# Five places reordered in a one-core hybrid transformer block

## The chip, the cores and the metric

The kernel runs on one core of one Trainium2 chip. The metric is device microseconds of one launch; a kernel's time is the median of its runs. The engines are named as in the profile: PE (TensorE) multiplies matrices, PEld is its weight load, DVE (VectorE) and ACT (ScalarE) do elementwise work, POOL (GpSimd) does some elementwise work and issues part of the transfers, and SP (SyncE) issues the rest. Each engine works through its own instruction queue in order, and the queues wait for each other through semaphores.

## The reference, cut to what matters

One block of a streaming encoder, for 1024 tokens of width 1024, all in float32:

```python
h = rmsnorm(x, norm_mix_g)
z = h @ w_in                       # one projection, then split
y_a = hgrn2(...)                   # gated recurrence, 4 heads of 128
y_b = fox(...)                     # forgetting attention, 8 heads of 64
y_c = memory(...)                  # attention into 256 memory tokens, 4 heads
gates = sigmoid(gate_logits)       # 3 branches x 1024
merged = sum_i gates_i * (y_i @ w_br_i)
x = x + merged @ w_out
h2 = rmsnorm(x, norm_ffn_g)
a, v = split(h2 @ w_up)            # 2 x 2816
y = gelu(causal_dwconv3(a) + b) * v
out = x + y @ w_down               # the "way down", 2816 -> 1024
```

## The kernel before, in words

Every float32 operand of a product is split into a high part, rounded to the matmul's own type (a cast on ACT, line 120), and a low part, the rest (a subtraction on DVE, line 128). A product is then three matmuls for each 128-deep slice (`mm3`, lines 114 to 116): high by high, high by low, low by high. The matrices are tiled in 128 rows by 512 columns, one bank of the accumulator memory each. Banks come from four rotating tags: `pp` (three), `lg` (two), `tr` (two) and `po` (one).

The large projections (pairs of projection chunks, the way up with `w_up` and the way down with `w_dn`) use a Winograd form of Strassen's scheme: seven products in place of eight for two by two blocks, on sums of blocks. One side's sums are made once and kept split ("families": B11, T1, T2, B22, T3, B21, T4); the other side's operands o1 to o7 are made anew for each unit. In one unit of the way up (`unit`) the products run in the order o1, o2, o3, o4, o5 (T3), o6 (B21), o7 (T4), and copies of half-finished banks (`snap`, line 1215) and final writes (`put`) go between.

The stages in order of time, with the places that the change touches:

- Start (0 to about 90 us): x is loaded in eight chunks `xk`. `x_chunk` makes the scaled and split operands `uh`, `ul` (lines 276, 277). The first two gate chunks and the memory's keys and values are projected meanwhile. `x_norm` squares the rows of x on ACT (line 356; the last one is `late["square"]`). `differences` (line 542) multiplies the eight chunks by their gains in place, on ACT, for the families.
- Dense pairs, then attention into memory and the forgetting attention (about 90 to 677 us). The attention's last head runs beside `hgrn_values`.
- HGRN2 (about 677 to 925 us): `hgrn_prep(h)` projects three things for a head in six halves of 24 matmuls. Each half is taken out of its bank by a multiplication on DVE into a tile `zt` (line 888), and a tanh on ACT writes it on (line 890). `hgrn_mix(h)` is the recurrence: exponentials on ACT, products of the key side on POOL (line 951), of the query side on DVE (line 952), small matmuls, and a norm whose power runs on POOL (`rstd_small`, line 133). The chunks of branch 1 run between the steps of the last head.
- The branches with their gates, `w_out`, the second norm, then the way up: `first_products` and `families` (lines 1285 to 1296) begin it; 22 units follow, with the results `yd` stored to memory.
- Way down: stages A11, S1, S2, S4, S3, A12, A22, each in six steps of up to two 128-deep slices. A step loads a weight and a `yd` piece (line 1406) and splits both (tiles `dwh`, `dwl`, `dbh`, `dbl`).

Space is taken from pools that are opened and closed like a stack. A tile that is laid over one from a closed pool waits for the last use of the old one. A tag has a fixed number of buffers that rotate in program order: `wl2` has five, `wh2` six, `rw` (raw weights of a unit) two, the gate tiles `gt` three (in the pool `gp`, open from the dense stage's end to the branches' end), `zt` one (in the pool `ph`, which lies over the attention's pools).

The order within each engine's queue is made by a scheduler that takes instructions by program order and priority as their inputs come free in its own model of time. `tc.issue_after(ins)` adds an edge without a wait: what the block issues on the engine of `ins` comes behind `ins` in that engine's queue. Instructions of other engines in the block are not bound by it.

The part of the way up's opening that the change adds to:

```python
for name, q, after in (("B22", 3, None), ("T3", 1, "e5"), ("B21", 2, "snap"), ("T4", 0, "snap")):
```

Of the kernel before, what the change touches and what calls it, by code (L numbers as in the profile page):

```python
# [8 lines left out]
F32 = mybir.dt.float32  # L9
# [5 lines left out]
P = 128  # L15
# [55 lines left out]
def tile_block(ctx: ExitStack, tc: tile.TileContext, xT, memT, x_rows, mem_rows, vec, fbias, mats, hmask, w_cm, w_hi, w_fqk, w_fv,  # L71
# [45 lines left out]

    def cast(eng, out, in_):
        if eng is S:
            S.copy(out, in_)  # L120
        elif eng is V:
            V.tensor_copy(out, in_)
        else:
            G.tensor_scalar(out, in_, 1.0, 0.0, ALU.mult, ALU.add)
# [5 lines left out]
    def rstd_small(out, ss, n):  # L130
        w = ss.shape[1]
        V.tensor_scalar(out, ss, 1.0 / n, EPS, ALU.mult, ALU.add)
        G.tensor_tensor(out, out, mhalf[:, :w], ALU.pow)

    wsplit = [S, V]

# [399 lines left out]
    def differences():  # L536

        b = []
        for k in range(4):
            for t in (k, k + 4):  # L540
                with tc.issue_after(late["square"].ins) if t > 3 else nullcontext():
                    S.activation(xk[t], xk[t], AF.Copy, scale=col(C_GX + t))
            b.append([xk[k + 4 * c][:, n * HB:(n + 1) * HB] for c in range(2) for n in range(2)])
        for k, (b11, b12, b21, b22) in enumerate(b):
            V.tensor_sub(b11, b11, b12)
            family_block("T1", k, b11)
        yield
        with tc.issue_after(first_gates.ins):
            for k, (t1, b12, b21, b22) in enumerate(b):
                V.scalar_tensor_tensor(out=t1, in0=t1, scalar=-1.0, in1=b22, op0=ALU.mult, op1=ALU.subtract)  # L550
                family_block("T2", k, t1)
        yield
        with tc.issue_after(first_gates.ins):
            for k, (t2, b12, b21, b22) in enumerate(b):
                V.tensor_sub(b12, b22, b12)
                family_block("T3", k, b12)
        yield
        for k, (t2, b12, b21, b22) in enumerate(b):
            V.scalar_tensor_tensor(out=t4[k], in0=t2, scalar=-1.0, in1=b21, op0=ALU.mult, op1=ALU.subtract)
        pxk.release()  # L560
        home["raw"] = tc.alloc_tile_pool(name="ps2", bufs=1, side="left", reuse_waits="tile")
        new_family(home["raw"], "T4")
        for k in range(4):
            family_block("T4", k, t4[k])
        yield
# [312 lines left out]
    def hgrn_prep(h):  # L878
        ph = state["ph"]
        qt = ph.tile([P, T], F32, tag="hq", name=f"hq_{h}", bufs=2)  # L880
        at = ph.tile([P, T], F32, tag="ha", name=f"ha_{h}", bufs=2)
        gz = ph.tile([P, T], F32, tag="hz", name=f"hz_{h}", bufs=2)
        for what, base, dst in ((0, 4, at), (1, 0, qt), (2, 8, gz)):

            for n, ps in cm_chunk(w_cm[base + h], KC, uh, ul, h == 3 and what == 2):
                sl = slice(n * HB, (n + 1) * HB)
                zt = ph.tile([P, HB], F32, tag="zt", name="zt")
                V.tensor_mul(zt, ps, rx[:, sl])  # L888
                d = dst[:, sl]
                S.activation(d, zt, AF.Tanh, scale=0.5)  # L890
                if what == 0:

                    G.tensor_scalar(d, d, TMIN, c1[:, h:h + 1], ALU.max, ALU.mult)
                else:

                    V.scalar_tensor_tensor(out=d, in0=d, scalar=1.0, in1=zt, op0=ALU.add, op1=ALU.mult)
                yield
        hset[h] = (qt, at, gz)
# [3 lines left out]
    def hgrn_mix(h, ya):  # L902
# [7 lines left out]
        for n in range(2):  # L910
# [103 lines left out]
            rr = ph.tile([P, 4], F32, tag="rr", name="rr", bufs=2)  # L1014
            S.activation(o2, po.rearrange("p (b v) -> p b v", b=4), AF.Square)
            V.reduce_sum(rr, o2, axis=AX.X)
            rstd_small(rr, rr, 4 * P)
            for b in range(4):
                S.activation(o2[:, b, :], po[:, b * P:(b + 1) * P], AF.Copy, scale=rr[:, b:b + 1])
            ptr = ps_tr()  # L1020
# [81 lines left out]
    yc = [[py.tile([P, T], F32R, tag=f"yc{p}{c}", name=f"yc{p}{c}") for c in range(4)] for p in "hl"]  # L1102
    for c in range(4):
        for t, d in zip(yc, ycd):
            G.dma_start(t[c], d[:, c, :].bitcast(F32R))
    run_all(branch(0, yh, yl))
    run_all(branch(2, *yc))
    mh, ml = [], []
# [31 lines left out]

    def operand_parts(h, src):
        l = pl.tile([P, HB], F32R, tag="wl2", name="wl2", bufs=5)
        late["split"] = split(S, h, l, src)
        return h, l

    def first_operands():
# [95 lines left out]
        V.tensor_add(t, a, b)  # L1242
        return t

    def unit(src, put, begun=None, before=None, after=None):


        raw = pw.tile([P, 4, HB], F32, tag="rw", name="rw", bufs=2)
        for i in range(2):
            late["raw"] = G.dma_start(raw[:, 2 * i:2 * i + 2, :], src[:, 2 * i:2 * i + 2, :])  # L1250
        a11, a21, a22, a12 = (raw[:, i, :] for i in range(4))
        if begun:
            x, y, e1, e5, e2, o4 = begun
            o5, o6, o7 = operand(sum_of(3, a11, a21)), operand(a12), operand(a22)
            before()
        else:
            with tc.issue_after(after.ins) if after else nullcontext():
                o1 = operand(a11)
                s1 = sum_of(1, a21, a22)
                o2 = operand(s1)  # L1260
            s2 = sum_of(2, s1, a11)
            x, y, e1, e5, e2 = first_products(o1, o2, operand(s2))
            o4 = operand(sum_of(4, s2, a12))
            o5 = operand(sum_of(3, a11, a21))
        product(y, o4, "B22", False)
        put(0, 1, y, e2)
        if not begun:
            o6 = operand(a12)
        product(x, o5, "T3", False)
        put(1, 1, x, e5)  # L1270
        if not begun:
            o7 = operand(a22)
        z = ps_tr()
        product(z, o6, "B21", True)
        put(0, 0, z, e1)
        product(x, o7, "T4", False)
        put(1, 0, x, None)
# [4 lines left out]
    def families():  # L1282

        for name, q, after in (("B22", 3, None), ("T3", 1, "e5"), ("B21", 2, "snap"), ("T4", 0, "snap")):
            with ExitStack() as order:
                if after:
                    order.enter_context(tc.issue_after(late[after].ins))
                if after == "snap":
                    order.enter_context(tc.issue_after(late["split"].ins))
                for k in range(4):  # L1290
                    late["last"] = family_block(name, k, quarters(k)[q])
            if name == "T3":
                spread(r2, rt2)
        px.release()
        late["pq"] = tc.alloc_tile_pool(name="pq", bufs=1, side="right", reuse_waits="tile")
# [14 lines left out]
                yield  # L1310

    sums = weight_sums()

    for p in range(NF // 2):
        at = []
# [51 lines left out]
                V.tensor_mul(dst, src, dst)  # L1367
            SP.dma_start(yd[:, 2 * c + n, p, :], dst)

        unit(w_up[2 * p + 1], put_v, after=None if p else late["last"])  # L1370
        for _ in range(1 + (1 <= p < 4)):
            next(sums, None)
        t1 = pq.tile([P, HB], F32, tag="ft", name="ft")
# [64 lines left out]
    for a, b, own, first, c, n, sign, last, xq in (  # L1438
# [4 lines left out]
        if not own and first:  # L1443
            ybanks = [ps_lg(), ps_lg(), ps_tr(), ps_tr()]
        dst = banks if own else ybanks
        end = a == "A22"
        held = []
        for i, ks in enumerate(steps):
            eng = G if a == "A11" else SP
            ops = [*parts("w", fetch("w", i, a, eng=eng)), *parts("b", yside(b, i, eng))]  # L1450
            if i == 4 and xq:
                with tc.issue_after(late["sp"].ins) if "sp" in late else nullcontext():
                    x_quarter(*xq)
            held.append((ks, *ops))
            if end and ks is steps[-2]:
                continue
            for m in range(4):
                for kk, h1, l1, h2, l2 in held:
                    for j in range(kk.stop - kk.start):
                        k = kk.start + j  # L1460
                        ms = slice(m * P, (m + 1) * P)
                        mm3(dst[m], h1[:, j, ms], l1[:, j, ms], h2[:, j, :], l2[:, j, :],
                            first and k == 0, k == NP - 1, not first)
                if ks.stop == NP:
                    j, sl = m + 4 * c, slice(n * HB, (n + 1) * HB)
                    d = xb[:, j, sl]
                    (V.tensor_add if sign > 0 else V.tensor_sub)(d, d, dst[m])
                    if last:
                        SP.dma_start(outT[:, j, sl], d)
            held = []  # L1470
# [110 lines left out]
```

## Time and profile before

| what | value |
|---|---|
| runs (3) | median 1764.69 us, 1764.61 to 1765.21 |
| the profiled execution | 1764.18 us |
| its span, first to last instruction | 1762.4 us |
| mean granted PE clock | 0.996 |
| PE busy | 1736.2 us, 99% |
| DVE busy | 1185.8 us, 67% |
| ACT busy | 786.7 us, 45% |
| POOL busy | 334.7 us, 19% |

The profile is one execution. "Busy" counts an engine's instructions; matmuls are pipelined, so a busy PE need not be at its peak. In the view of waits a line says who waited for whom, for how long in total, how often, and the longest time. In the timeline a line has the start, the duration, the engine, the line of the code, the operation, output and input tiles, sizes, and in brackets how long the engine stood idle before and what ended that. In the view of windows each engine has its busy time and number of instructions in a stretch; PEclk is the granted share of TensorE's full clock there.

### The profile page before, as it was taken

How to read it: one execution, taken by the hardware profiler on the slowest of the kernel's cores; microseconds unless marked ns; L12 is line 12 of the kernel's file. 1: busy time of each engine (PE TensorE's matmuls, PEld its weight loads, DVE VectorE, ACT ScalarE, POOL GpSimd, SP SyncE). 2: the span in 40 equal slices, each digit the busy share in tenths (PEclk: the TensorE clock that was granted, in tenths of full speed). 3: DMA queues.
4: the chain of work that ended last, by engine and by line, in shares of the span. 5: the costliest groups of instructions: out<-in, count | busy, mean ns of one | idle time of the engine just before them, and what ended most of it. 6: DMA issues, size and time to landing. Idle time of an engine off the chain costs nothing.

```text
span 1762.4 us, 24530 instructions
## 1 busy us (share of the span) xinstructions
PE 1736.2 (99%) x9069; PEld 1471.4 (83%) x9069; DVE 1185.8 (67%) x2181; ACT 786.7 (45%) x1318; POOL 334.7 (19%) x431
## 2 busy tenths in 40 slices
PE   8999999999999999999989999999999999999998
PEld 6778899989898997888878888788888888778887
DVE  7656445665756567778866755797777877674654
ACT  8633356545555554445331233543343443433332
POOL 1100032443424333334230000111111111100000
PEclk9999999999999999999999999999999999999999
DMA  9533232221212211001226452466454445494772
GB/s 361 178 119 105 83 128 73 76 95 60 91 47 85 84 46 52 25 31 56 77 78 216 153 200 80 136 188 163 139 160 133 119 128 152 144 362 145 238 269 84
DMA packets 83209, 227.36 MB, mean 129 GB/s; under 512 B 9600, under 2 KB 12424, under 8 KB 83088
## 3 DMA queue, kind: packets, MB, share of 16 engines
q1 hardware_dynamic: 65040, 161.29, 26.1%
q0 software_dynamic: 18048, 64.50, 12.6%
q8 instruction: 71, 1.16, 0.3%
q14 instruction: 50, 0.41, 0.1%
HBM read 180.88 MB, written 67.93 MB: 141 GB/s over the span
## 4 chain that ended last, share of the span: by engine, by line
PE 97%; ACT 1%; DVE 1%; DMA 0%; issue 0%; SPq 0%; POOL 0%; DVEq 0%; ACTq 0%
PE pp L115 21%; PE pp L116 21%; PE pp L114 21%; PE lg L115 4%; PE lg L116 4%; PE lg L114 4%; PE tr L114 2%; PE tr L115 2%; PE tr L116 2%; PE lg L970 2%; PE po L836 1%; PE lg L795 1%; PE lg L794 1%; PE po L835 1%; PE po L116 1%; PE po L114 1%
## 5 line engine op out<-in xcount | busy, mean ns | idle before, releaser
L115 PE MATMUL pp<-ul,wh 128*128 128x512 f32 x412 | 165.6, 402 | 0.0
L116 PE MATMUL pp<-uh,wl 128*128 128x512 f32 x412 | 165.4, 401 | 0.0
L114 PE MATMUL pp<-uh,wh 128*128 128x512 f32 x412 | 163.2, 396 | 1.5 <-DVE zt L888 1.5
L115 PE MATMUL pp<-wl,uh 128*128 128x256 f32 (+1 forms) x512 | 145.7, 285 | 0.0
L116 PE MATMUL pp<-wh,ul 128*128 128x256 f32 (+1 forms) x512 | 145.3, 284 | 0.0
L114 PE MATMUL pp<-wh,uh 128*128 128x256 f32 (+1 forms) x512 | 144.7, 284 | 0.0
L120 ACT CAST wh<-s 128x512 fp32r<-128x512 f32 x113 | 68.4, 619 | 152.8 <-PE pp L115 76.8
L120 ACT CAST wh<-raw 128x1024 fp32r<-128x1024 f32 (+2 forms) x76 | 67.5, 890 | 98.9 <-PE pp L115 86.9
L1250 POOL DMA_DIRECT2D rw<-in_w_up x44 | 24.1, 554 | 403.4 <-ACT sqs L1185 169.9
L114 PEld LDWEIGHTS pp<-wh,uh 128*128 128x128 f32 x512 | 96.4, 189 | 1.2
L116 PEld LDWEIGHTS pp<-wh,ul 128*128 128x128 f32 x512 | 96.5, 189 | 0.9
L115 PEld LDWEIGHTS pp<-wl,uh 128*128 128x128 f32 x512 | 96.4, 188 | 0.9
L120 ACT CAST dwh<-wr 128x1024 fp32r<-128x1024 f32 (+1 forms) x42 | 41.1, 980 | 124.6 <-PE tr L115 41.7
L120 ACT CAST wh<-rw 128x512 fp32r<-128x512 f32 x83 | 50.6, 619 | 101.2 <-PE pp L115 59.7
L114 PEld LDWEIGHTS pp<-uh,wh 128*128 128x128 f32 x412 | 78.4, 190 | 17.5 <-DVE zt L888 1.7
L115 PEld LDWEIGHTS pp<-ul,wh 128*128 128x128 f32 x412 | 77.9, 189 | 16.8
L116 PEld LDWEIGHTS pp<-uh,wl 128*128 128x128 f32 x412 | 77.9, 189 | 15.5
L128 DVE TENSOR_TENSOR wl<-raw,wh 128x1024 fp32r<-128x1024 f32 (+2 forms) x76 | 78.4, 1033 | 17.9 <-ACT wh L120 12.7
L128 DVE TENSOR_TENSOR wl<-s,wh 128x512 fp32r<-128x512 f32 x113 | 77.0, 683 | 8.9 <-ACT wh L120 8.9
L128 DVE TENSOR_TENSOR wl<-rw,wh 128x512 fp32r<-128x512 f32 x83 | 55.7, 686 | 29.5 <-PE pp L116 14.1
L951 POOL TENSOR_TENSOR X<-X,kt 128x256 f32<-128x256 f32 x48 | 50.4, 1057 | 124.5 <-ACT X L950 119.5
L128 DVE TENSOR_TENSOR dwl<-wr,dwh 128x1024 fp32r<-128x1024 f32 (+1 forms) x42 | 47.6, 1133 | 39.0 <-ACT dwh L120 39.0
(471 smaller groups left out, 5185.7 us busy)
## 6 DMA issues: line engine op xcount, KB each, us to landing
rw<-in_w_up POOLq DMA_DIRECT2D x44, 512.0 KB, 4.6
sd<-in_w_dn POOLq DMA_DIRECT2D x30, 512.0 KB, 5.9
br<-yd SPq DMA_DIRECT2D x30, 512.0 KB, 5.3
raw<-in_w_cm SPq DMA_DIRECT2D x26, 512.0 KB, 3.4
gd<-gt SPq DMA_DIRECT2D x48, 256.0 KB, 2.0
gt<-gd SPq DMA_DIRECT2D x48, 256.0 KB, 2.8
yd<-fc SPq DMA_DIRECT2D x44, 256.0 KB, 2.5
wr<-sd SPq DMA_DIRECT2D x20, 512.0 KB, 4.4
```

The lines of the kernel that those rows point to most:

```text
L114: PE.matmul(ps, lh, rh, start=first, stop=False, skip_group_check=more)
L115: PE.matmul(ps, lh, rl, start=False, stop=False, skip_group_check=more)
L116: PE.matmul(ps, ll, rh, start=False, stop=last, skip_group_check=more)
L120: S.copy(out, in_)
L128: return (sub or V).tensor_sub(l, src, h.bitcast(F32))
L794: PE.matmul(ps[:, :w], qa[i][:, tsl], kh[i][:, s0:s0 + w], start=True, stop=False)
L795: fox_sets[p][3] = PE.matmul(ps[:, :w], qa[i][:, tsl], kl[i][:, s0:s0 + w], start=False, stop=True)
L835: PE.matmul(o, vhl[:, sb, :], ph[:, src], start=(sb == 0), stop=False)
L836: PE.matmul(o, vhl[:, sb, :], pl[:, src], start=False, stop=last)
L951: G.tensor_mul(Xk, Xk, Kv[:, :, 0, :])
L970: PE.matmul(o[:, b * 64:(b + 1) * 64], X[:, b * P:(b + 1) * P], Xq[:, b * bpb:(b + 1) * bpb, :], start=True, stop=True)
L1250: late["raw"] = G.dma_start(raw[:, 2 * i:2 * i + 2, :], src[:, 2 * i:2 * i + 2, :])
```

## The change

Five edits, from the first place in time to the last:

1. The in-place scalings of x (line 542): before, those of chunks 4 to 7 stood behind the last square in ACT's queue; now all eight do.
2. `hgrn_prep(0)`: its six copies `zt` go to gate tiles (three buffers, already open) in place of the one `zt` buffer of the pool `ph`. Heads 1 to 3 keep `zt`.
3. The eight loads of the memory branch's operands `yc` (line 1105, POOL's queue) are put behind the last power of the HGRN2 norm (`state["norm"]`) in POOL's queue.
4. In the way up's opening, ACT's casts of family B21 come behind the cast of o5, and those of T4 behind the cast of o7.
5. In the last unit of the way up, between products T3 and B21, a new function `down_operands` loads the pieces of the way down's first step (two loads on POOL's queue into an `rw` buffer) and splits them as four operands of 512 columns in `wh2` and `wl2`. The first step of stage A11 uses these and loads and splits nothing itself.

```diff
     def cast(eng, out, in_):
         if eng is S:
-            S.copy(out, in_)
+            return S.copy(out, in_)
...
         for k in range(4):
             for t in (k, k + 4):
-                with tc.issue_after(late["square"].ins) if t > 3 else nullcontext():
+                with tc.issue_after(late["square"].ins):
                     S.activation(xk[t], xk[t], AF.Copy, scale=col(C_GX + t))
...
-                zt = ph.tile([P, HB], F32, tag="zt", name="zt")
+
+                zt = ph.tile([P, HB], F32, tag="zt", name="zt") if h else gate_tile()
                 V.tensor_mul(zt, ps, rx[:, sl])
...
-            rstd_small(rr, rr, 4 * P)
+            state["norm"] = rstd_small(rr, rr, 4 * P)
...
         for t, d in zip(yc, ycd):
-            G.dma_start(t[c], d[:, c, :].bitcast(F32R))
+            with tc.issue_after(state["norm"].ins):
+                G.dma_start(t[c], d[:, c, :].bitcast(F32R))
...
         l = pl.tile([P, HB], F32R, tag="wl2", name="wl2", bufs=5)
-        late["split"] = split(S, h, l, src)
+        late["cast"] = cast(S, h, src)
+        late["split"] = V.tensor_sub(l, src, h.bitcast(F32))
...
-            o5, o6, o7 = operand(sum_of(3, a11, a21)), operand(a12), operand(a22)
+            o5 = operand(sum_of(3, a11, a21))
+            late["o5"] = late["cast"]
+            o6, o7 = operand(a12), operand(a22)
+            late["o7"] = late["cast"]
             before()
...
             o7 = operand(a22)
+        if ahead:
+            ahead()
         z = ps_tr()
         product(z, o6, "B21", True)
...
                 if after == "snap":
                     order.enter_context(tc.issue_after(late["split"].ins))
+                    order.enter_context(tc.issue_after(late["o7" if name == "T4" else "o5"].ins))
...
+    class Blocks:
+
+        def __init__(self, tiles):
+            self.tiles = tiles
+
+        def __getitem__(self, at):
+            return self.tiles[at[1]][:, at[2]]
+
+    def down_operands():
+
+        raw = pw.tile([P, 4, HB], F32, tag="rw", name="rw", bufs=2)
+        G.dma_start(raw[:, 0:2, :], w_dn[:, 0, 0:2, :])
+        G.dma_start(raw[:, 2:4, :], yd[:, 0, 0:2, :])
+        ops = [operand(raw[:, i, :]) for i in (0, 2, 1, 3)]
+        late["down"] = [Blocks([ops[i + 2 * j][q] for j in range(2)]) for i in range(2) for q in range(2)]
...
-        unit(w_up[2 * p + 1], put_v, after=None if p else late["last"])
+        unit(w_up[2 * p + 1], put_v, after=None if p else late["last"],
+             ahead=down_operands if p == NF // 2 - 1 else None)
...
-            ops = [*parts("w", fetch("w", i, a, eng=eng)), *parts("b", yside(b, i, eng))]
+            if a == "A11" and i == 0:
+                ops = late["down"]
+            else:
+                ops = [*parts("w", fetch("w", i, a, eng=eng)), *parts("b", yside(b, i, eng))]
```

More of the change, by code (lines that the diff above doesn't have):

```diff
@@ L132, in rstd_small @@
         V.tensor_scalar(out, ss, 1.0 / n, EPS, ALU.mult, ALU.add)
[L133 removed]
+        return G.tensor_tensor(out, out, mhalf[:, :w], ALU.pow)
     wsplit = [S, V]
@@ L1243, in sum_of, with unit @@
         return t
-    def unit(src, put, begun=None, before=None, after=None):
+    def unit(src, put, begun=None, before=None, after=None, ahead=None):
         raw = pw.tile([P, 4, HB], F32, tag="rw", name="rw", bufs=2)
```

## The prediction

> **What bounds the kernel now.** I read the page first, for the busy shares. PE is the bound, and at most 26 us of its span are not matmuls:
>
> ```profile
> span 1762.4 us, 24530 instructions
> ```
>
> ```profile
> PE 1736.2 (99%) x9069; PEld 1471.4 (83%) x9069; DVE 1185.8 (67%) x2181; ACT 786.7 (45%) x1318; POOL 334.7 (19%) x431
> ```
>
> So a change of order gains only where PE waits. The second view is the list of PE's waits (who waited for whom, us in total, times, longest), whose six longest entries hold most of the idle time:
>
> ```profile
> PE tr L114 <- ACT wh L120: 5.8, 2, 5.3
> PE lg L970 <- POOL X L951: 4.5, 1, 4.5
> PE pp L114 <- ACT wh L120: 2.6, 1, 2.6
> PE pp L115 <- DVE dbl L128: 1.5, 1, 1.5
> PE pp L114 <- DVE zt L888: 1.5, 1, 1.5
> PE po L114 <- ACT gh L120: 1.4, 1, 1.4
> ```
>
> The first is the wait for the first operand after the start, which nothing here touches. The others are five places, each waiting once. Four of them answer to edits 1, 2, 4 and 5; the 4.5 us for POOL's product lie near edit 3.
>
> Third, windows laid behind these places show a second price. The number after POOL's is the granted clock:
>
> ```profile
> 678.31:681.72 3.41, 3.41 (x9) 2.63 (x10) 1.47 (x3) 1.14 (x2) 2.80 (x2) 0.50 0.56 168
> 907.00:913.83 6.83, 6.20 (x30) 6.20 (x31) 2.80 (x5) 1.62 (x5) 2.53 (x3) 0.50 0.01 2
> 1545.30:1548.71 3.41, 3.31 (x8) 2.63 (x9) 3.41 (x5) 0.00 (x0) 1.61 (x3) 0.50 1.01 359
> 1123.10:1126.51 3.41, 3.41 (x23) 3.15 (x24) 3.41 (x6) 2.68 (x5) 0.64 (x2) 1.00 0.20 82
> ```
>
> Behind the `zt` wait and behind the `dbl` wait PE ran 3.41 us at half clock, so each lost 3.41 x 0.5 = 1.7 us more; behind POOL's product it was 6.83 us, a loss of 3.4. The last row lies behind the 2.6 us wait, at full clock: whether a wait trips the clock is not decided by its length alone.
>
> [...]
>
> **Edit 1, scalings of x.** Three of the eight scalings run on ACT between 15 and 25 us, the third directly ahead of the cast for which PE waits:
>
> ```profile
> 15.00:25.00 10.00, 3.34 (x3) 1.00 1.03 410
> ```
>
> ```profile
> 23.96 1.14 ACT L542 ACTIVATE xk<-xk,cv 128x1024 f32<-128x1024 f32 x1
> 25.00 1.03 ACT L120 CAST gh<-raw 128x1024 fp32r<-128x1024 f32 x1
> ```
>
> Its source, the issue on SP and the time from issue to landing of this tile's loads:
>
> ```profile
> 13.84 0.33 SPq L139 DMA_DIRECT2D raw<-in_w_cm  x1
> ```
>
> ```profile
> DMA to landing us min/median/max: 6.6/8.7/10.1
> ```
>
> Without them ACT comes to the cast 3.3 us sooner, at about 21.7. Its source was issued at 13.84 and lands 6.6 to 10.1 us later, so between 20.4 and 23.9, at the median at 22.5. At the median the cast is 2.5 us earlier and the whole 1.4 us wait goes; at the late end 25.0 - 23.9 = 1.1 us are gained. I take 1.4, with ends 1.1 and 1.4. The four scalings that move behind the squares add 4 x 1.1 = 4.4 us to ACT's queue there. What they delay is the cast of T1, and PE has a second pair of gate halves and a product on unsplit chunks to run before the first T1 product, so I cost this at nothing; if that cover is gone it costs up to 4.4 us. Late next: `gl`.
>
> **Edit 2, copies in gate tiles.** PE had finished three halves of `hgrn_prep(0)`, which fill all three `pp` banks, and could not begin a fourth: the first copy out ran only after the attention's last instruction. In the last stretch of the attention PE so had no filler:
>
> ```profile
> PE tr L823 <- DVE pl L128: 0.6, 1, 0.6
> PE po L836 <- DVE pl L128: 0.3, 1, 0.3
> ```
>
> ```profile
> 677.48 0.67 DVE L888 TENSOR_TENSOR zt<-pp,rx 128x512 f32<-128x512 f32 x1
> ```
>
> Three gate tiles let three halves be copied out while the attention runs, and so free 72 matmuls of filler. The waits 0.6 + 0.3 + 1.5 = 2.4 us are a hole of some 11 matmuls (eight at half clock in 3.41 us make 0.21 us each at full clock). They go, and with them the half clock, 1.7: 4.1 us. The tanh still writes into `ph` and still waits for the attention. Does the recurrence's chain follow, or does PE's lead run into it?
>
> ```profile
> 683.77 0.63 ACT L890 ACTIVATE hq<-zt 128x512 f32<-128x512 f32 x1 [3.57 <-DVE zt L888]
> 684.42 1.28 ACT L909 ACT_TABLE_LOAD   x1
> 685.72 1.15 ACT L909 ACTIVATE L<-ha,c 128x1024 f32<-128x1024 f32 x1
> ```
>
> ```profile
> 678.92 3.99 POOL L893 TENSOR_SCALAR ha<-ha,c 128x512 f32<-128x512 f32 x2 [10.82 <-ACT ha L890]
> ```
>
> L needs POOL's `ha`, done at 678.92 + 3.99 = 682.9, yet it started at 685.72, behind `hq`, which waited 3.57 us for a copy, and a table load. With the copy at hand L can start at 683, 2.8 us earlier, and PE's lead of 4.1 us meets it with 1.3 us too much, part of which the chain's slack takes. I take 3.5, with ends 0 (the chain takes all back) and 4.1. Moved past: the gate loads of branch 1, which use the same three buffers, now come after these copies; they are wanted two heads later, and cost nothing.
>
> **Edit 3, loads of the memory branch.** The loads already stand behind the last power in POOL's queue, with the power finished when the first is issued:
>
> ```profile
> 919.35 1.01 POOL L133 TENSOR_TENSOR rr<-rr,mhalf 128x4 f32<-128x4 f32 x1 [9.82 <-DVE rr L132]
> 920.31 0.65 POOL L1105 DMA_DIRECT2D ych<-ychd  x1
> ```
>
> The edge fixes an order that is there: 0. The 4.5 us wait comes from a product that took 3.38 us, not from a load:
>
> ```profile
> 903.33 3.38 POOL L951 TENSOR_TENSOR X<-X,kt 128x256 f32<-128x256 f32 x1 [2.36 <-ACT X L950]
> ```
>
> ```profile
> L951 POOL TENSOR_TENSOR X<-X,kt x48: 726/938/4343, 692.0 to 908.7; 128x256 f32<-128x256 f32 x48
> ```
>
> **Edit 4, casts of the way up.** The cast of o5 (`wh<-s`) stands behind eight family casts:
>
> ```profile
> 1117.79 0.59 ACT L1215 COPY fe<-pp 128x512 f32<-128x512 f32 x1 [1.58 <-PE pp L116]
> 1118.27 2.18 ACT L120 CAST B21h<-x 128x512 fp32r<-128x512 f32 x4
> 1120.35 2.17 ACT L120 CAST T4h<-x 128x512 fp32r<-128x512 f32 x4
> 1122.43 0.62 ACT L120 CAST wh<-s 128x512 fp32r<-128x512 f32 x1
> ```
>
> ```profile
> 1117.56 0.69 DVE L1242 TENSOR_TENSOR s<-rw 128x512 f32<-128x512 f32 x1
> ```
>
> ```profile
> 1123.66 1.95 PE L295 MATMUL tr<-ident,rt 128*128 128x128 f32 x16
> ```
>
> The row behind these four is its sum on DVE, ready at 1118.25, so the cast can run at 1118.4 and its low part be there by 1119.7. PE came to T3 when the cast ended, at 1123.05, after waiting 2.6 us, so it was free at 1120.4: the whole 2.6 us go. What waits now: B21 and T4, by up to three casts (o5, o6, o7; 0.52 us apart as in the groups of four), 1.6 us. B21's casts end at 1118.4 + 1.6 + 2.2 = 1122.2 and its last subtraction at most 1.3 us later, 1123.5; PE first runs T3 (12 x 0.21 = 2.6 us) and the spread of the norm (the last row, 1.7 us of it alone), until about 1124.7. That covers it; without this cover the 1.6 us show. I take 2.6, with ends 1.0 and 2.6.
>
> **Edit 5, the way down's first operands.** PE begins the way down with three products on high parts and then waits for DVE, which comes from the last writes of the way up and only then makes `dwl` and `dbl`:
>
> ```profile
> 1542.39 0.69 DVE L1365 SCALAR_TENSOR_TENSOR fc<-pp,fc 128x512 f32<-128x512 f32 x1 [0.59 <-PE pp L116]
> 1542.99 1.22 DVE L128 TENSOR_TENSOR dwl<-wr,dwh 128x1024 fp32r<-128x1024 f32 x1
> 1544.13 1.22 DVE L128 TENSOR_TENSOR dbl<-br,dbh 128x1024 fp32r<-128x1024 f32 x1
> ```
>
> ```profile
> PE pp L114 <- DVE fc L1365: 0.3, 1, 0.3
> PE pp L114 <- DVE fe L1362: 0.3, 1, 0.3
> ```
>
> The two subtractions (2.4 us) become four of 0.69 ahead of the last products. The first step is 24 matmuls, 5.1 us from about 1542.2, in which DVE makes the second step's pair from 1542.99 on, done at 1545.4 for a use at 1547.3. So the waits 1.5 + 0.3 (for `fc`, a bank that the first step can take last) and the half clock's 1.7 go: 3.5 us; the 0.3 for `fe` stays. Nothing else must be late: the fourth operand needs the `wl2` buffer of o6, free when product B21 ends, and DVE has T4's 2.6 us left for one subtraction and the three writes it had there. The loads:
>
> ```profile
> 1511.56 0.69 DVE L128 TENSOR_TENSOR wl<-rw,wh 128x512 fp32r<-128x512 f32 x1 [1.79 <-PE pp L116]
> ```
>
> This is about where the `rw` buffer comes free, so the loads (as many as the first step issued before) leave at 1512, some 20 us before use; behind them in POOL's queue stand a sum of weights and the other steps' loads, all wanted later. On SP the T1 loads must wait until the first step has read its tiles, about 5 us longer; they have a whole stage as cover. I take 3.5, with ends 0 (DVE as late as before) and 3.8 (the `fe` wait filled too).
>
> **The sum.** 1.4 + 3.5 + 0 + 2.6 + 3.5 = 11.0 us. The profiled execution took 1764.18 us, 1.8 over its span; the median of the runs, 1764.69, is 0.5 above it. Its own time becomes 1753.2, the median 1764.7 - 11.0 = 1753.7.
>
> **The rivals.**
> - The chain of HGRN2 takes back PE's lead of edit 2: 1757.2. For it: the chain's head moves only by what L gains. Against it: the six longest waits, quoted first, hold only one of that stage behind its opening, the one at its end, so the chain has slack.
> - POOL's starved product goes. If the new order of DVE's instructions lets it run in its median 0.94 us, the 4.5 us and the 3.4 of the clock go too: 1753.7 - 7.9 = 1745.8. [...]
> - DVE stays the bound at the way down, since four more subtractions meet its last writes: 3.5 back, 1757.2.
> - The clock drops move to other waits: the 2.6 us wait tripped none, shorter ones did, so its moment matters. One or two drops kept: 1755.4 to 1757.1.
> - Slower: the same starvation, more often. HGRN2's last head ends without filler, and there a starved product costs 7.9 us. With the stage's order shifted by edit 2, one more gives 1761.6; from two more on (1769.5) the change loses. For it: the longest product in this trace took 4.34 us and stood elsewhere, where PE had filler. Against it: the median of 48 is 0.94.
> - That an edit does nothing is certain only for edit 3, and is in the sum.
>
> **How the numbers follow.** The forecast has 0.45, 1753.7 with a range of its own of 1750 to 1757 from the ends of edits 1 and 4 and a scheduler that reorders a little; HGRN2 taking back 0.15; the starved product gone 0.12; the way down 0.08; the clock 0.05: all faster by over 0.2% (3.5 us, about what a measurement can tell from none), 0.85. Two of these together end within 0.2%: 0.05. Slower 0.10. The range goes from 1744, just below the starved product's case, to 1761, where edits 2 and 5 both gain nothing.
>
> **What would show it.** Among PE's waits those for `gh`, `zt`, `dbl` and the 2.6 us for `wh` are gone; half clock remains only near 907; o5's cast stands right after the snap; two loads into `rw` stand near 1512; ACT has no L542 before the last square. Wrong would be: a new wait over 2 us in HGRN2 or at the way down, or a first T1 product that waits for ACT.

## The result: no faster, and slightly slower

| | before | after |
|---|---|---|
| median of 9 runs each, us | 1764.74 (1763.16 to 1767.85) | 1768.15 (1767.34 to 1771.25) |
| profiled execution: span, us | 1762.4 | 1767.6 |
| granted clock, mean | 0.996 | 0.995 |

The ratio of after to before is 1.0017, with a 95% interval of 1.0006 to 1.0029: about 3 us slower, where 11 us less were forecast. By the 0.2% bound of the prediction that is "within", by the interval it is a small loss. These are the first lines of the profile after (span; busy time of each engine, with its share):

```profile
span 1767.6 us, 24539 instructions
...
PE 1738.7 (98%) x9069; PEld 1474.4 (83%) x9069; DVE 1184.5 (67%) x2183; ACT 789.3 (45%) x1320; POOL 335.4 (19%) x431
```

PE has the same 9069 matmuls. Its list of waits after the change (who waited for whom, us in total, times, longest):

```profile
PE lg L971 <- DVE X L953: 9.5, 2, 5.0
PE tr L114 <- ACT wh L120: 5.8, 2, 5.0
PE pp L116 <- DVE fa L1345: 1.6, 1, 1.6
PE pp L114 <- DVE zt L889: 1.3, 1, 1.3
PE pp L114 <- ACT fe L427: 1.2, 1, 1.2
PE tr L1023 <- ACT o L1020: 1.2, 1, 1.2
PE lg L114 <- DVE gt L381: 1.1, 1, 1.1
```

All four waits that the change was meant to remove are gone: `gh` (1.4), `zt` at the attention's end (1.5; the 1.3 us now on the list stands at another place, 836 us), `wh` on the way up (2.6) and `dbl` (1.5). In their place stand two waits of about 5 us for `X`, where there was one of 4.5, and five of 1.1 to 1.6 us. A new wait over 2 us in HGRN2 was one of the prediction's own signs of being wrong. The half clock moved too. Between the start and the last matmul it stood before at 678, 907 and 1545 us (13.7 us in all); after, in windows laid on it (the number 0.50 is the granted clock), only behind the two waits for `X`, but for 17.1 us:

```profile
899.73:906.56 6.83, 6.20 (x28) 6.23 (x29) 5.03 (x13) 2.98 (x7) 2.28 (x3) 0.50 0.00 1
916.79:927.03 10.24, 8.99 (x42) 9.02 (x43) 5.08 (x11) 1.62 (x5) 1.47 (x2) 0.50 0.01 2
```

So the change has to be read by stages. Three stages can be cut out of every trace by the same matmuls: A, from the start to the first FoX product with `qa`; B, from there to the first product of the way up (`B11`); C, from there to the end of the last matmul. Edit 1 lies in A, edits 2 and 3 in B, edits 4 and 5 in C.

| us | A | B | C | sum |
|---|---|---|---|---|
| before | 335.1 | 772.4 | 650.4 | 1757.9 |
| after | 337.3 | 780.9 | 644.8 | 1763.1 |
| difference | +2.3 | +8.5 | -5.6 | +5.2 |

The sum is the difference of the two spans. C gained nearly what edits 4 and 5 were to bring; B lost more than that.

**Where B's 8.5 us went.** Two windows of each trace, with the matmuls into the projection banks `pp` alone (the first number in brackets is their count). The first runs from the first product of FoX's attention to its last; the second from the first product of HGRN2's recurrence to its last transpose. Before:

```profile
335.07:676.69 341.62, 261.50 (x1422) 211.91 (x1420) 13.78 (x20) 17.39 (x37) 1.00 0.20 68
690.04:926.05 236.01, 160.03 (x640) 117.77 (x640) 23.23 (x34) 0.00 (x0) 0.99 0.17 55
```

After:

```profile
337.33:690.80 353.47, 275.81 (x1481) 222.81 (x1480) 15.82 (x23) 17.38 (x37) 1.00 0.19 65
703.98:936.81 232.83, 141.95 (x569) 104.65 (x569) 21.03 (x31) 0.00 (x0) 0.96 0.16 52
```

The attention holds 59 more of these matmuls and is 11.9 us longer (353.47 - 341.62). The recurrence has 71 fewer beside it: 18.1 us of PE's busy time left it (160.03 - 141.95), but it became only 3.2 us shorter. It goes by its own chain through DVE, ACT and POOL, and where the filler has run out PE waits for that chain. That is the two waits for `X`, in the last head.

Why did the recurrence not begin earlier, as I had forecast? The timeline before has, at the attention's last product and at the recurrence's first:

```profile
676.42 0.28 PE L836 MATMUL po<-pl,vhl 128*128 128x128 f32 x1
...
690.05 0.65 PE L931 MATMUL lg<-qq,kt 128*128 128x192 f32 x3
```

After:

```profile
690.52 0.28 PE L836 MATMUL po<-pl,vhl 128*128 128x128 f32 x1
...
691.11 1.15 ACT L891 ACTIVATE ha<-gt 128x512 f32<-128x512 f32 x2
...
692.17 0.62 ACT L891 ACTIVATE hq<-gt 128x512 f32<-128x512 f32 x1
...
694.87 0.63 ACT L891 ACTIVATE hq<-gt 128x512 f32<-128x512 f32 x1
695.40 0.62 ACT L891 ACTIVATE hz<-gt 128x512 f32<-128x512 f32 x1
...
698.06 0.64 ACT L891 ACTIVATE hz<-gt 128x512 f32<-128x512 f32 x1 [2.04 <-DVE gt L889]
698.71 1.28 ACT L910 ACT_TABLE_LOAD   x1
700.01 1.16 ACT L910 ACTIVATE L<-ha,c 128x1024 f32<-128x1024 f32 x1
...
703.99 0.65 PE L932 MATMUL lg<-qq,kt 128*128 128x192 f32 x3
```

The tanh writes into `ph`, memory that the attention frees, so no step of the chain behind the copies can run before the attention's last product, in either kernel. From that product to `L` were 9.3 us before (676.42 to 685.72, a row of the prediction) and are 9.5 after; to the recurrence's first product 13.6 and 13.5. With all six copies at hand, the scheduler put all six tanh ahead of `L` on ACT (the four of `hq` and `hz` among them, which `L` doesn't need; ACT sat 2.04 us idle for the copy of the last), so `L` gained nothing; and the matmuls put into the attention moved everything behind it by their own length.

The sums agree. PE's waits between 690 and 940 us are 5.5 us before (4.5 + 0.8 + 0.2) and 12.6 after (9.5 + 1.3 + 1.2 + 0.6); half clock there costs (17.1 - 6.8) x 0.5 = 5.1 us more. That is 12.2 us lost, against the 4.1 us that the prediction counted at the attention's end and that did come: 8.1 us, where B shows 8.5.

### The profile page after: what moved, and what is told of

It is laid out like the page before. It is cut to its first block, busy times and chain, and to the rows that moved or that the text cites. A ratio compares the mean times of both kernels' runs of the same rounds, so it can differ in the third digit from the quotient of the medians.

```text
span 1767.6 us, 24539 instructions
## 1 busy us (share of the span) xinstructions
PE 1738.7 (98%) x9069; PEld 1474.4 (83%) x9069; DVE 1184.5 (67%) x2183; ACT 789.3 (45%) x1320; POOL 335.4 (19%) x431
## 5 line engine op out<-in xcount | busy, mean ns | idle before, releaser
L810 ACT ACTIVATE pt<-pt,st 128x128 f32<-128x128 f32 (+3 forms) x64 | 49.7, 777 | 39.9 <-DVE st L807 32.8
L812 POOL TENSOR_SCALAR pt<-pt,st 128x128 f32<-128x128 f32 (+3 forms) x64 | 51.7, 808 | 77.6 <-DVE st L811 60.9
```

The lines of the kernel that those rows point to most:

```text
L810: S.activation(pt[:, :ns], pt[:, :ns], AF.Exp, bias=st[:, 2:3], accum_out=st[:, 3:4])
L812: G.tensor_scalar(pt[:, :ns], pt[:, :ns], st[:, 3:4], 0.0, ALU.mult, ALU.add)
```

## The experiments

Eleven kernels in three groups, each group beside the kernel before. "1p" is another form of edit 1, told below. The ratio has its own interval and isn't always the quotient of the two medians; where they differ, the interval decides.

| kernel | median, us | before beside it | ratio, 95% interval | A | B | C |
|---|---|---|---|---|---|---|
| all but edit 2 | 1759.73 | 1764.66 | 0.9972 (0.9960 to 0.9985) | 337.1 | 771.1 | 644.9 |
| edits 2 and 3 | 1772.70 | 1764.66 | 1.0043 (1.0027 to 1.0059) | 336.4 | 780.2 | 651.9 |
| edit 1 | 1765.17 | 1764.66 | 1.0000 (0.9991 to 1.0010) | 337.2 | 772.6 | 650.5 |
| edits 4 and 5 | 1759.34 | 1764.66 | 0.9970 (0.9956 to 0.9984) | 335.5 | 772.2 | 644.9 |
| one copy in a gate tile | 1767.41 | 1766.44 | 1.0011 (1.0001 to 1.0021) | 334.8 | 776.1 | 648.8 |
| two copies | 1773.93 | 1766.44 | 1.0041 (1.0026 to 1.0056) | 339.9 | 779.5 | 650.3 |
| two copies, matmuls held | 1766.82 | 1766.44 | 1.0002 (0.9992 to 1.0013) | 339.1 | 772.1 | 650.3 |
| edits 1p, 4 and 5 | 1761.05 | 1766.44 | 0.9969 (0.9957 to 0.9980) | 334.6 | 774.7 | 644.9 |
| edit 4 | 1764.34 | 1764.38 | 0.9997 (0.9985 to 1.0009) | 336.6 | 772.1 | 649.3 |
| edit 5 | 1762.37 | 1764.38 | 0.9979 (0.9967 to 0.9991) | 336.5 | 770.8 | 646.0 |
| edits 4, 5, products on VectorE | 1761.79 | 1764.38 | 0.9977 (0.9964 to 0.9990) | 338.3 | 772.4 | 644.9 |

A trace is one execution, and its stages have a spread of their own. The kernel before and the eight rows without an edit in A run from 334.8 to 339.9 us there; the six without an edit in B (the kernel before among them) lie between 770.8 and 774.7, five of them below 772.7. So a difference of 2 us in A says nothing, one of 4 us in B little, and one of 7 or more is read as the edit's. C isn't free of it either: the six traces without an edit there run from 648.8 to 651.9 us.

Most of this spread is half clock. With 0.5 us taken off for each us of half clock in the stage (1.7 for a stretch of 3.41), the six in B come to 767.0 to 767.9 us, the six in C to 648.5 to 648.8, and the nine in A to 334.8 to 336.6. These corrected times are estimates, but they show what the order of the work costs apart from the clock, and they are used below beside the measured ones.

### Edit 2 undone, and edit 2 done alone

All edits but the second; the diff is against the changed kernel:

```diff
-                zt = ph.tile([P, HB], F32, tag="zt", name="zt") if h else gate_tile()
+                zt = ph.tile([P, HB], F32, tag="zt", name="zt")
```

> All edits but 2: the first head's six copies go back to their tile zt, edits 1, 3, 4 and 5 stay. Theory F (filler spent early): with gate tiles 72 more of the first head's projection matmuls are issued among the attention's last head, the attention ends 14 us later (676.7 to 690.8 us), and the last head of HGRN2 is left without other work, where two waits of about 5 us and 17 us of half clock stand now; stage by stage the changed kernel lost 8.5 us between the attention's start and the first product of the way up. Then this kernel is 8.5 us below the changed one: about 1759.5 us, 5 us under the kernel before, with the attention's end back at 679 us and the two waits of 5 us at the projection of the last head gone. Rival G (edit 1's later scalings or edit 3's later loads of yc made the loss): this kernel stays within 2 us of the changed one, 1766 to 1770 us, and the two waits stay.

Edits 2 and 3 alone, against the kernel before:

```diff
-                zt = ph.tile([P, HB], F32, tag="zt", name="zt")
+                zt = ph.tile([P, HB], F32, tag="zt", name="zt") if h else gate_tile()
...
+            with tc.issue_after(state["norm"].ins):
+                G.dma_start(t[c], d[:, c, :].bitcast(F32R))
```

> Edits 2 and 3 alone. Theory F: attention's end 14 us later, branch 1 begins about 12 us earlier, two waits of about 5 us on VectorE at the projection of the last head with half clock behind them; 8.5 us above the kernel before, some 1773 us. The prediction's reading (the moved matmuls fill a hole that stood open): 3.5 us below, 1761 us. Rival G: within 1 us of the kernel before.

Measured: 1759.73 us without edit 2, 4.9 us under the kernel before and 8.4 under the changed one; 1772.70 us with edits 2 and 3 alone, 8.0 above. B is 771.1 and 780.2. In the waits between 660 and 940 us, without edit 2:

```profile
PE lg L970 <- POOL X L951: 4.5, 1, 4.5
PE pp L114 <- DVE zt L888: 1.5, 1, 1.5
```

and with edits 2 and 3 alone:

```profile
PE lg L970 <- DVE X L952: 9.4, 2, 5.0
PE pp L114 <- DVE zt L888: 1.3, 1, 1.3
```

The loss belongs to edits 2 and 3, and the two long waits come and go with it. Rival G (edit 1 or the later loads) falls for edit 1. Edit 3 wasn't tried alone; the two copies of the next section have the loss without it.

### How much of it, and by what: copies one by one, and matmuls held back

The kernel before, with the first one or the first two of the six copies in gate tiles (`k` is 1 or 2):

```diff
-                zt = ph.tile([P, HB], F32, tag="zt", name="zt")
+                zt = gate_tile() if h == 0 and 2 * (what, n)[0] + n < k else ph.tile([P, HB], F32, tag="zt", name="zt")
```

> The kernel before, with the first of the first head's six copies alone in a gate tile; the other five keep zt. In PE's written order 24 more projection matmuls then stand ahead of the attention's last product (57 with all six), and 35 instead of 44 between it and the recurrence's first product. Theory F as a price for every matmul moved ahead: a third of the loss of edits 2 and 3 alone (8.0 us), some 2.7 us more, 1767 us. Theory F with a hole (the first 24 fill the 3 us in which PE stood idle at the attention's end, 676.4 to 678.2 us and before it; only what is moved beyond that delays the recurrence): attention's end 3 to 4 us later, the recurrence's first product at 688 to 692 us (690.0 before), no half clock at 678 us, and the kernel at 1762 to 1765 us. Rival G (gate tiles held by the copies delay the gates' loads): the loss of 8 us is there with one tile too, 1771 us or more.

> The first two copies in gate tiles: 48 more matmuls ahead of the attention's last product, 38 between it and the recurrence's first product. Price per matmul: two thirds of 8.0 us, 1770 us. With a hole of 3 us: attention's end 8 us later (685 us), the recurrence's first product 4 to 6 us later (694 to 696 us), 1767 to 1769 us. Rival G: 1771 us or more, as with one copy.

Two copies in gate tiles as well, but the matmuls of the last three halves queued on PE behind the attention's last product:

```diff
+                    late["fox"] = PE.matmul(o, vhl[:, sb, :], pl[:, src], start=False, stop=last)
...
-    run_all(hgrn_prep(0))
+    first = hgrn_prep(0)
+    for _ in range(3):
+        next(first)
+    with tc.issue_after(late["fox"].ins):
+        run_all(first)
```

> The first two copies in gate tiles, as in the run beside it, but the matmuls of the first head's last three halves are held behind the attention's last product, so the order ahead of the attention's end is that of the kernel before; 62 matmuls instead of 44 stand between it and the recurrence's first product. Theory F: the attention ends at 677 us again, its waits at the end stay or shrink by 1.5 us, and the recurrence's first product is at 691 to 694 us (44 matmuls took 13.3 us with the idle time among them, 62 take 14.2 us and more); the loss is at most that delay, 1764 to 1768 us. Rival G: the gate tiles are used as in the run beside it, so the time is the same as there.

Measured, on one chip: one copy 1.0 us above the kernel before (B +3.7), two copies 7.5 above (B +7.1), two copies with the matmuls held 0.4 above, no difference (B -0.3). The windows with `pp` alone, for two copies:

```profile
339.86:691.04 351.18, 273.24 (x1470) 220.77 (x1468) 15.14 (x22) 17.38 (x37) 1.00 0.20 66
701.50:937.89 236.39, 149.80 (x598) 109.74 (x598) 22.58 (x33) 0.00 (x0) 0.96 0.17 53
```

and with the matmuls held:

```profile
339.13:680.86 341.73, 261.66 (x1423) 212.14 (x1422) 15.14 (x22) 17.39 (x37) 1.00 0.20 66
695.09:929.81 234.72, 157.40 (x622) 114.01 (x622) 23.21 (x34) 0.00 (x0) 0.98 0.17 53
```

The two kernels use the same tiles. What differs is where three halves of matmuls stand on PE, and that is worth 7.1 us. So for two copies the cause is the place of the matmuls, not the tiles or their loads; that it is the same with all six copies, where the same two long waits stand, is argued from this.

Is there a price for each matmul moved? B grows with the count moved ahead of the attention's end: 24 matmuls +3.7 us (within the spread), 48 +7.1, all of them (59 by the windows, 57 in PE's written order) +7.8. But the 3.7 us with one copy are half clock, of which B held 17.1 us in place of 10.2:

```profile
705.32:708.73 3.41, 3.41 (x14) 3.02 (x13) 1.89 (x6) 1.26 (x2) 1.77 (x2) 0.50 0.40 150
906.71:920.36 13.65, 10.23 (x48) 10.26 (x49) 7.90 (x18) 3.34 (x9) 2.53 (x3) 0.50 0.01 1
```

B of edits 1p, 4 and 5, which no edit touches, held 17.1 us of it too. With half of it taken off, B is 767.3 us before, 767.6 with one copy, 770.9 with two, 767.0 with two and the matmuls held, and 771.7 to 772.4 with all six. By these estimates the first 24 matmuls cost nothing and the next 24 cost 3.3 us; an even price per matmul isn't shown. How much of the half clock belongs to the edit isn't separated either. The times don't settle it: one copy is 1.0 us above by the medians, 0.2 to 3.7 by the interval. Neither finer form of theory F came out whole. A price per matmul said 2.7 and 5.3 us, a hole filled by the first 24 no loss and then 2.3 to 4.3 us; two copies cost 4.6 to 9.9 us by the interval. With one copy and with two PE's wait of 1.5 us at the attention's end was still there, since the next copy again needs `zt`. Counted from the attention's first product, the recurrence began 2.0 us later than before with one copy and 6.7 with two.

The held kernel also shows that removing the wait at the attention's end is worth nothing by itself here: its waits between 660 and 940 us have no `zt`, yet its recurrence starts 1.0 us later than before, counted from the attention's first product (695.09 - 339.13 against 690.04 - 335.07), and the times are equal.

### Edit 1 alone, and in another form

```diff
-                with tc.issue_after(late["square"].ins) if t > 3 else nullcontext():
+                with tc.issue_after(late["square"].ins):
```

> Edit 1 alone. Theory R (the row of x's norm waits behind the scalings): ScalarE's eight scalings now stand ahead of its copy of rx_row, which the gates and the dense product's first operands need, so the wait at gh (1.4 us) goes, but new waits of 0.7 to 1.6 us come at 69, 80, 88 and 92 us; the first matmul of the FoX projections comes 2.3 us later and the kernel takes about 1767 us. The prediction's reading: 1.4 us less, 1763.3 us. Between them, no difference, if what was lost before the attention is taken up by its later waits on transfers.

Measured 1765.17 us, ratio 1.0000. The wait at `gh` is gone, and the measured time is not less. ACT's timeline before:

```profile
52.54 4.26 ACT L542 ACTIVATE xk<-xk,cv 128x1024 f32<-128x1024 f32 x4
...
59.81 0.25 ACT L285 COPY rx_row<-tr 8x128 f32<-8x128 f32 x1
```

and with edit 1 alone:

```profile
51.84 1.06 ACT L356 ACTIVATE xr<-xr 128x1024 f32<-128x1024 f32 x1 [0.76 <-DMA xr<-in_x_rows]
...
52.90 8.43 ACT L542 ACTIVATE xk<-xk,cv 128x1024 f32<-128x1024 f32 x8
...
63.30 0.25 ACT L285 COPY rx_row<-tr 8x128 f32<-8x128 f32 x1
```

Eight scalings instead of four now stand between the last square and `rx_row`, the row of the norm that all gates are multiplied with, and it comes 3.5 us later. ACT could not come to its squares earlier either: the last one waited for its row to be loaded. What the edit freed between 15 and 25 us went into that wait and was paid back at the scalings. No gain is measured, but the interval (0.9991 to 1.0010) reaches down to 1.6 us less, so the 1.4 us that were forecast aren't excluded. Theory R's loss of 2 us isn't shown by the times either. The traces lean to a small loss: the three with edit 1 have A at 337.1 to 337.3 us with no half clock in it, the nine without it at 334.8 to 336.6 with the clock taken off.

The other form queues the first four scalings behind the second gate cast, so that four, not eight, stand behind the squares:

```diff
-            S.copy(out, in_)
+            late["cast0"] = S.copy(out, in_)
+            return late["cast0"]
...
+        late["gate1"] = late["cast0"]
...
-                with tc.issue_after(late["square"].ins) if t > 3 else nullcontext():
+                with tc.issue_after(late["square" if t > 3 else "gate1"].ins):
```

> Edits 4 and 5 with another form of edit 1: the scalings of chunks 0 to 3 are queued behind the second gate cast instead of behind the last square, so four scalings as before, not eight, stand between the last square and the copy of rx_row. Theory R: the wait at gh (1.4 us) goes, nothing comes back at 69, 88 and 92 us, the first product with T1 is where it was or earlier, and the kernel is 1.4 us under edits 4 and 5 alone, 1757.9 us. Rival: the time ahead of the attention is set by transfers and the rows of x (ScalarE waited 1.6 and 0.8 us for rows with edit 1), then the wait goes and comes back somewhere else, 1759 us. Either is near the limit of what the times tell; the stages in the trace decide.

Measured: ratio 0.9969, the same as edits 4 and 5 alone (0.9970). Of PE's waits ahead of 60 us, the 1.4 us at `gh` had become this one, for the cast of a memory weight that now stood behind the scalings:

```profile
PE pp L114 <- ACT wh L120: 2.0, 1, 2.0
```

The rival was right that the wait comes back somewhere else. It had named transfers and the rows of x; here the wait moved along ACT's queue. ACT is busy with work that PE wants all through this stretch (before, 43.1 of the 45.0 us from 15 to 60 us), so putting four scalings elsewhere in it chooses which of PE's operands is late.

### Edits 4 and 5

Both together, then each alone; their diffs are those of the change.

> Edits 4 and 5 alone. From the stages of the changed kernel: edit 4 takes away 2.8 us at the last quarters of the way up and gives 1.8 us back at a wait for the next unit's sum (1 us in all), edit 5 takes away 3.9 us: 4.9 us below the kernel before, 1759.8 us. The prediction's own terms gave 6.1 us: 1758.6 us. Rival: the gains of these joints hang on the shift of everything ahead of them (transfers that land later relative to the work); then the kernel is less than 3 us faster.

> Edit 4 alone. The prediction's term: 2.6 us less, 1762 us on the scale of 1764.7 for the kernel before. From the stages of edits 4 and 5 together: the gap of 3.00 us ahead of T3 (start to start) goes, and a gap of 2.05 us comes at the next unit's first product, where PE waits for VectorE's low part of that unit's first operand, which is queued behind the four T4 subtractions (they end 1.1 us earlier than before, not 2.6 us): about 1 us less, 1763.7 us, and the same trade in the trace.

> Edit 5 alone. The prediction's term: 3.5 us less with the half clock behind the wait counted apart. From the stages of edits 4 and 5 together: 3.9 us less, about 1760.8 us, the wait at dbl (1.5 us) gone and no half clock near 1545 us. Rival: edit 5 gains only beside edit 4; then less than 1.5 us.

Together 5.3 us under the kernel before, ratio 0.9970. In C, edit 4 alone is 1.1 us less, edit 5 alone 4.4, both 5.5. Of edit 5's 4.4 us, 1.7 are the half clock near 1545 us, and whether that drop comes is in part chance: the kernel with one copy kept the same wait of 1.5 us for `dbl` and ran on at full clock behind it. With the clock taken off, C is 648.7 us before, 647.6 with edit 4, 646.0 with edit 5 and 644.9 with both: 1.1, 2.7 and 3.8 us less, so they add up, and the rival that edit 5 gains only beside edit 4 falls. The times are less sharp. Edit 5 alone is 2.0 us under the kernel before by the medians and 3.7 by the ratio (0.9979, interval 0.9967 to 0.9991, or 1.6 to 5.8 us), and its profiled execution was among its fastest. The interval of edit 4 alone holds no difference (0.9985 to 1.0009). Its trade is in the timeline of edits 4 and 5, at the next unit's first product:

```profile
1126.36 2.49 DVE L128 TENSOR_TENSOR T4l<-x,T4h 128x512 fp32r<-128x512 f32 x4
...
1128.77 0.69 DVE L1243 TENSOR_TENSOR s<-rw 128x512 f32<-128x512 f32 x1
1129.37 0.69 DVE L1144 TENSOR_TENSOR wl<-rw,wh 128x512 fp32r<-128x512 f32 x1
...
1130.01 0.07 DVE L1343 MEMSET fa<- 128x2 f32 x2
1130.11 0.49 PE L116 MATMUL pp<-B11h,wl 128*128 128x512 f32 x1 [1.65 <-DVE fa L1343]
```

The profile names `fa`, the fill of 0.07 us. But the product reads `wl`, and `wl` was done at 1130.06, 0.05 us before it. So PE waits for DVE, which comes straight from T4's four subtractions; that reading is argued from the rows, and no run moved `wl`.

Edit 5 alone leaves no wait of PE between 1500 and 1600 us in the list, and PE is busy throughout at full clock:

```profile
1540.00:1550.00 10.00, 10.00 (x45) 8.14 (x44) 7.25 (x9) 4.03 (x5) 1.08 (x2) 1.00 0.59 216
```

### Is the wait for X GpSimd's?

The long wait is marked with POOL's product before and with DVE's after. With edits 4 and 5, the last head's products of X with `kt` went from POOL to DVE, from the second level on:

```diff
-                G.tensor_mul(Xk, Xk, Kv[:, :, 0, :])
+                (V if h == 3 and n == 1 and li > 0 else G).tensor_mul(Xk, Xk, Kv[:, :, 0, :])
```

> Edits 4 and 5, and in the last head's second half the products of X with kt on VectorE instead of GpSimd, from the second level on (four or five products of 0.4 us each more on VectorE). This prices the wait that edit 2 doubled. Theory W (the wait of 4.5 us is GpSimd's product, which took 3.38 us there beside a median of 0.94): the wait shrinks to 1 or 2 us, the half clock of 6.8 us behind it goes or shrinks, 3 to 6 us less than edits 4 and 5 alone, 1753.5 to 1756.5 us. Rival: VectorE is the bound of that stretch (it is busy nearly all of 900 to 909 us), the wait goes over to its own products and the time stays within 1.5 us of edits 4 and 5, or rises.

Measured 1761.79 us, ratio 0.9977 against 0.9970 with the product on POOL: no gain. B is 772.4 against 772.2. Between 880 and 930 us PE waited just as long, now for DVE:

```profile
PE lg L970 <- DVE X L952: 4.6, 1, 4.6
```

So theory W's gain didn't come: with POOL out of it, DVE's own queue sets the same moment. Since the edit also gives DVE more to do, it doesn't separate what set the moment before. But the held kernel left the product on POOL, and there the profile puts the same wait, 4.8 us, down to DVE. I read it as a wait for the recurrence's chain in a stretch without filler, whichever engine comes last; that is argued, not shown.

## Why the prediction was wrong, step by step

- **The sum**: 11.0 us less were forecast; 3.4 us more were measured. Edit 2's term is the one that failed, by 12 us: 3.5 less forecast, 8.0 to 8.5 more measured. The other terms together were 7.5, and all edits but the second measured 4.9.
- **Edit 2, "and so free 72 matmuls of filler"**: the working had both numbers, a hole of 11 matmuls and 72 to fill it, and never asked where the other 61 would stand. Ahead of the attention's last product stood 59 more, and they made the attention 11.9 us longer.
- **Edit 2, "L can start 2.8 us earlier"**: it started as late as before, counted from the attention's last product (9.5 against 9.3 us), behind three more tanh than before, which without `zt` now stood ahead of it in ACT's queue.
- **Edit 2, "with ends 0 ... and 4.1"**: the lower end of 0 excluded a loss without a reason. This is the step that failed: that the moved matmuls would be missing beside the recurrence's chain had no term in the sum, and it measured 7 to 8 us. The step "the tanh still writes into `ph` and still waits for the attention" was right, and was the reason for a loss: what is put in front of the attention's end delays the chain.
- **Edit 1, "I cost this at nothing"**: the cover I named was for T1's cast. The copy of `rx_row`, in the same queue behind the same scalings, was overlooked. No gain was measured where 1.4 was forecast, though the interval just reaches it.
- **Edit 3, 0**: not tried alone. Nothing contradicts it.
- **Edit 4, 2.6 with ends 1.0 and 2.6**: the wait went as worked out; 1.1 us came of it in the trace, and no difference clear of noise in the times. The term looked at B21 and T4 but not at what stands behind T4 on DVE, the next unit's first operand.
- **Edit 5, 3.5**: the mechanism was right. In C it measured 4.4, the half clock's 1.7 and the small waits for `fc` and `fe` included. That the clock's part came is luck: without it 2.7 remain, and the ratio says 3.7 (1.6 to 5.8).
- **The rivals**: the slower one came nearest. It had a second wait of the same kind in the last head, 7.9 us with the clock, and the place was right. Its mechanism was not: it took the wait for POOL's product, starved now and then, and gave it a chance of 0.10. That DVE's order starves the product was an assumption of mine that no run shows: before, the product of 3.38 us at 903.33 lies beside 3.32 us of DVE's work, but one at 900.24 us took 0.73 us with DVE at work all through it. The cause is the filler that edit 2 spends early, and the long waits are put down to DVE in POOL's place. "POOL's starved product goes" rested on the same reading; with the product on DVE it did go, and the wait stayed at 4.6 us.
- **The half clock**: that a wait's length alone doesn't decide was right. Counting 1.7 us at `zt` as a sure gain was not: the kernels with all but edit 2 and with edit 5 alone keep that wait of 1.5 us and ran on at full clock behind it. The same holds for the 1.7 us at `dbl`.

The fastest versions are edits 4 and 5, all but edit 2, and edits 1p, 4 and 5, each about 5 us under the kernel before beside it (0.9969 to 0.9972). No run here shows one better than another.

## What to carry to other kernels

Filler matmuls are a budget: a wait that is filled by drawing work forward is filled at the cost of the place where that work used to stand. So count what a freed buffer lets through, not only whether it fills the hole, and ask whether the moved work stands ahead of the event at which a latency-bound chain begins. Where a buffer's release is to help one step, hold the other work back with an edge of its own, as in the held kernel, and read the queue of the engine that the moved step lands on down to the next thing that PE needs.

## What the runs showed of the chip that I had not expected

The same wait of 2.6 us on the way up was followed by full clock in one trace and by half clock in another. The kernel before, in two windows that share the wait (PE's busy time is the second number, then the clock):

```profile
1118.64:1122.05 3.41, 1.86 (x9) 1.18 (x7) 0.00 (x0) 3.41 (x8) 2.46 (x3) 1.00 0.75 249
1122.05:1125.47 3.42, 2.37 (x19) 2.29 (x20) 2.40 (x4) 3.14 (x6) 0.00 (x0) 1.00 0.52 212
```

1.55 and 1.05 us were idle, and the clock stayed full; in the prediction's row, from 1123.10 to 1126.51 us, it was full still. The held kernel, in a window that has the whole wait and in the one behind it:

```profile
1123.77:1127.18 3.41, 0.81 (x4) 0.37 (x3) 0.33 (x1) 3.41 (x7) 1.13 (x2) 1.00 0.96 356
1127.18:1130.59 3.41, 3.41 (x16) 3.27 (x15) 3.41 (x7) 1.79 (x4) 0.94 (x2) 0.50 0.12 47
```

2.60 us were idle, and the next 3.41 us ran at a granted clock of 0.50. So neither the kind of a wait nor its length alone decides, and what does isn't shown by these runs. The 1.7 us behind a short wait (3.41 x 0.5, an estimate from these rows) are to be counted as a chance. Executions of one kernel differ by such amounts: among those of the kernel before, beside the last group, one took 1761.92 us at a mean granted clock of 0.998, another 1769.57 at 0.993.
